# Two reorderings in a hybrid trunk's attention part: first differences of V behind weight splits, and ada sums handed out at other places

## The chip, the cores and the metric

One core of a Trainium2 chip runs the whole program. The metric is the device time of one execution in microseconds (us); three runs of the kernel before gave a median of 1159.88 us (1157.45 to 1161.33). Engines are called by their names: TensorE (PE, with its weight loads PEld), VectorE (DVE), ScalarE (ACT), GpSimd (POOL), and SyncE (SP), which here only issues transfers.

## The reference

The kernel computes two layers on 512 tokens of width 1024, in float32. Layer 0 mixes tokens by stick-breaking attention with 16 heads of 64, layer 1 by a gated token-mixing MLP; each is followed by a SwiGLU block. Every sub-layer has a norm before and behind it and a shift, a scale and a gate computed from a conditioning vector c. The part that matters here:

```python
def ada_modulation(c, w, b):
    m = jax.nn.silu(c) @ w + b
    shift, scale, gate = jnp.split(m, 3, axis=-1)
...
        log_beta = jax.nn.log_sigmoid(z)
        log_1m = jnp.where(before, jax.nn.log_sigmoid(-z), 0.0)
        later = lax.cumsum(log_1m, axis=3, reverse=True) - log_1m
        a = jnp.where(before, jnp.exp(log_beta + later), 0.0)
        outs.append(jnp.einsum('bhts,bhsd->bhtd', a.astype(v.dtype), v[:, :, :kend]))
...
        shift, scale, gate = ada_modulation(c, mix_ada_w[i], mix_ada_b[i])
        h = rms_norm(x, mix_pre_g[i]) * (1.0 + scale) + shift
        y = stick_breaking_mixer(h, sb_w_qkv[j], sb_w_o[j])
        x = x + gate * rms_norm(y, mix_post_g[i])
```

The weights `a` of one row are differences of neighbouring running products of sigmoid(-z). The kernel moves that difference to the other factor: it multiplies the running products with the first differences of V along the tokens.

## The kernel before, in words

**Products in three parts.** A float32 factor is split into a high part that TensorE's fast format holds (`h`, made by ScalarE as a copy) and the rest (`l`, made by VectorE as source minus high part). `mm3` (L104) multiplies high by high, high by low and low by high. Every weight tile of 512 KB goes the same way: SyncE loads it into `raw` (a ring of two buffers), ScalarE makes `wh` (L159, or L154 for the q and k weights of head pairs 1 to 7) and VectorE makes `wl` (L160 or L155) into a ring of five. A `raw` buffer is free for the next load when `wl` has read it. `wget` emits the splits some tiles ahead of use.

**Helpers and lines.** `mm` (L93) records nearly every matmul and `transpose` (L101) the rest. The class `Vector` (L62) passes VectorE's operations on, so most of VectorE's rows have L69; `split` gives ScalarE's rows with L116. While `pe["chain"]` or `dve.chain` is set, each operation on that engine is ordered behind the one before it, so the written order is the executed one. `order` (L85) adds such an order between two instructions without a semaphore.

**Stages around the change.** First come the norm, the turning of h and the ada sums of the first sub-layer (to 61 us or so), mixed with the first half of V (columns 0 to 511) and the q and k of head pair 0. The second half of V follows (the loop over k, L958): eight steps of 12 matmuls (`v_step`), weights for two steps in one tile, with the scores `z` of head pair 0 between them (blocks named B31, B2 and B0). Then 3 + 8 + 9 steps of the filler, then eight head pairs. The filler yields after each eighth of a q or k product for a later pair (banks `pqk`); `fill(n, at)` takes n such steps.

**First differences.** `u_steps` takes the four token tiles of one half of V in the order 2, 3, 0, 1. For each, GpSimd issues a transfer that copies the tile one token up into `vs` (one buffer, L635 and L637); VectorE subtracts (L644); ScalarE and VectorE split the result into U's two parts. The next copy reuses `vs`, so it starts when U's low part is written. The first half's four steps stand in the loop of V's second half, after k = 1, 3, 5 and 7. V's first half is kept for this in `vf`, two tiles of the pool `npool`, which has two buffers; so is the second half afterwards.

**A head pair.** `scores` makes z, ScalarE's sigmoid writes `ga`, and VectorE's scan makes the running products `left`. `flip` transposes them (`tw`), ScalarE and VectorE split them into `ar`, and `values` multiplies with U into `av`. `gather` and `part` make the output `of` and its split `o`. Filler steps stand between these.

**Ada sums.** `Bg` computes a gate G, a scale A and a shift B for coming sub-layers, a stage at a time. There are eight multiply-add stages each on VectorE over 128x1024 (tile `rawada`, loaded by SyncE), then a split of the sum in two halves (`acch`, `accl`) and, after a pause of one stage, two matmuls with ones for each half; here they write into the scores' first bank, `z`. `ada_step` runs the next stage of G and, when G is through, of A and B. G's tiles lie in the pool of 28 slots, A's and B's in a pool with two buffers. Stages are handed out at k = 2, 4, 6, inside `fill(..., 1)` after the second filler step, and once more per pair from pair 4 on; what is left is run after the pairs.

Of the kernel before, what the change touches and what calls it, by code (L numbers as in the profile page):

```python
# [31 lines left out]
def trunk(ctx: ExitStack, tc: tile.TileContext, A: dict, out: bass.AP):  # L32
    nc = tc.nc
# [5 lines left out]
    npool = ctx.enter_context(tc.tile_pool(name="npool", bufs=2))  # L39
# [37 lines left out]
    dve = Vector()  # L77
# [43 lines left out]
    turn = [-1]  # L121
    wpools = [(wpool, 5)]
    fwork = {}

    raws = []

    def wload():

        src, a, b, key = stream[len(raws)]
        if src is None:  # L130
            raws.append(block_loads(key[1]))
            return
        raw = wraw.tile([P, a, b], F32, tag="raw", name=nm("raw"))
        load(raw[:], src)
        raws.append(raw)

    def wemit():
        n = len(got)
        src, a, b, key = stream[n]
        if len(raws) == n:  # L140
            wload()
        if src is None:
            if len(raws) == n + 1 < len(stream) and stream[n + 1][0] is None:
                wload()
            got.append(blocks(*raws[n]))
            return
        raw = raws[n]
        if key[0] == "wdn" and key[2] in SEVEN[key[1]]:
            got.append(down_blocks(raw))
            return  # L150
        h, l = wtile(a, b)
        if key[0] == "wqk" and key[1]:

            act.activation(h[:], raw[:], AF.Copy)  # L154
            nc.vector.tensor_tensor(l[:], raw[:], h[:].bitcast(F32), ALU.subtract)  # L155
            if len(raws) == n + 1 and stream[n + 1][3][0] == "wqk":
                wload()
        else:
            act.activation(h[:], raw[:], AF.Copy)  # L159
            nc.vector.tensor_tensor(l[:], raw[:], h[:].bitcast(F32), ALU.subtract)  # L160
        got.append((h, l))

    def wtile(a, b):
        turn[0] = (turn[0] + 1) % sum(c for _, c in wpools)
        pool = wpools[0][0] if turn[0] < wpools[0][1] else wpools[1][0]
        return (
            pool.tile([P, a, b], F32R, tag="wh", name=nm("wh")),
            pool.tile([P, a, b], F32R, tag="wl", name=nm("wl")),
        )
# [405 lines left out]
    def ada_step(n=1):  # L575
        bg.step(bg0.step(n))
# [42 lines left out]
            a, b = hTk(hT, k, tt * P, P)  # L619
            mm3(vb[tt][:], a, b, w[0][:, k % 2, :], w[1][:, k % 2, :], k == 0, k == KD - 1)  # L620

    def v_evac(vb):
        vf = [npool.tile([P, 2, 512], F32, tag="n", name=nm("vf")) for _ in range(2)]
        vf = [vf[tt // 2][:, tt % 2, :] for tt in range(NT)]
        for tt in range(NT):
            act.activation(vf[tt], vb[tt][:], AF.Copy)
        return vf

    def u_steps(vf, hf, pool):

        def shifted(tt):
            vs = pool.tile([P, 512], F32, tag="vs", name=nm("vs"))
            if tt == NT - 1:
                nc.gpsimd.memset(vs[96:P, :], 0.0)
            nc.gpsimd.dma_start(out=vs[0 : P - 1, :], in_=vf[tt][1:P, :])  # L635
            if tt < NT - 1:
                nc.gpsimd.dma_start(out=vs[P - 1 : P, :], in_=vf[tt + 1][0:1, :])  # L637
            return vs

        turns = (2, 3, 0, 1)  # L640
        vs = shifted(turns[0])
        yield
        for n, tt in enumerate(turns):
            dve.tensor_tensor(vs[:], vs[:], vf[tt], ALU.subtract)  # L644
            src = vs[:].rearrange("p (a e c) -> p a e c", a=4, e=2)
            dst = U[hf][tt][:].rearrange("p a (q c) -> p a q c", q=4)
            split(dst[:, :, 0::3, :], dst[:, :, 1:3, :], src)
            if n + 1 < NT:
                vs = shifted(turns[n + 1])
            yield  # L650
# [75 lines left out]
    vb = [bank("v0") for _ in range(NT)]  # L726
# [36 lines left out]
    act.activation(ones_r, cc[:], AF.Copy)  # L763
    st0.__exit__(None, None, None)
    fwork["raw"] = ctx.enter_context(tc.tile_pool(name="wraw2", bufs=2))
    vf0 = v_evac(vb)
    o8 = []
    with tc.tile_pool(name="att", bufs=1) as att, tc.tile_pool(name="att2", bufs=2) as att2:

# [49 lines left out]
        def fill(n, at=None):  # L819
            for j in range(n):  # L820
                next(fgen, None)
                if at is not None and j == min(at, n - 1):
                    ada_step()


# [3 lines left out]
        for js in (B31, B2, B0):  # L829
            at, n = {}, 0  # L830
# [121 lines left out]
        early_u = u_steps(vf0, 0, att)  # L952
        next(early_u)
        vb = [bank("v1") for _ in range(NT)]
# [3 lines left out]
        for k in range(KD):  # L958
            if k % 2 == 0:
                wv = wget(("wv", 1, k // 2))  # L960
            v_step(vb, 1, k, wv)
            if k in (1, 4):
                cur[0](B31 if k == 1 else B2)
            if k in (2, 4, 6):
                ada_step()
            if k % 2:
                next(early_u)
        late_u = u_steps(v_evac(vb), 1, att)
        next(late_u)
        dve.chain = True  # L970
        tw = [bank("tw") for _ in range(2)]
        av = [bank("av") for _ in range(2)]
        fill(3, 1)
        cur[0](B0)
        for n in FIRST:
            fill(n, 2)
        for i in range(NPAIR):
            scores, flip, values, gather, part = cur
            more = i + 1 < NPAIR
            F = iter(FILLS if i < 5 else LAST[i - 5])  # L980
            flip(LATE, 0)
            flip(LATE, 1)
            if i:
                last_part()
            fill(next(F))
            if more:
                cur = attend(i + 1)
                cur[0](B31)
            fill(next(F), 1)
            values(LATE, 0, False)  # L990
            values(LATE, 1, False)
            fill(next(F))
            flip(EARLY[0], 0)
            flip(EARLY[0], 1)
            if i < 4:
                next(late_u)
            else:
                ada_step()
            fill(next(F))
            if more:  # L1000
                cur[0](B2)
            fill(next(F), 1)
            values(EARLY[0], 0, False)
            values(EARLY[0], 1, False)
            flip(EARLY[1], 0)
            flip(EARLY[1], 1)
            fill(next(F))
            if more:
                cur[0](B0)
            fill(next(F), 1)  # L1010
            values(EARLY[1], 0, True)
            values(EARLY[1], 1, True)
            gather()
            last_part = part
# [521 lines left out]
```

## Time and profile before

| | before |
|---|---|
| median of three runs | 1159.88 us |
| profiled execution, its own time | 1160.02 us |
| its span, first to last instruction | 1158.3 us |
| TensorE busy | 1124.4 us (97%) |
| VectorE busy | 932.9 us (81%) |
| ScalarE busy | 596.5 us (52%) |
| mean granted TensorE clock | 0.992 |

A row of the timeline gives start, duration, engine, line, operation, tile written <- tiles read, shapes and count, and in brackets how long the engine had been idle and what ended that idle time. A row of the waits gives engine, line and tile that waited, what for, the total in us, how often, and the longest. A row of the stretches gives a window, its length, each engine's busy time with its count of instructions, the granted clock (1.00 is full), the DMA engines' busy share and GB/s. Starts are in us from the span's start.

### The profile page before, as it was taken

What the parts mean: (1) busy time and instruction counts of PE and PEld (TensorE: products, weight loads), DVE (VectorE), ACT (ScalarE), POOL (GpSimd) and SP (SyncE); (2) the same over time, 40 slices, a digit from 0 to 9 for tenths busy, and PEclk for the clock granted to TensorE, in tenths of its full rate; (3) what the DMA queues carried; (4) which work ended last, traced back from release to release, by engine and by line L of the source; (5) the groups of instructions that cost most, each with busy time, mean ns of one, the idle gap of its engine ahead of it and who ended that gap; (6) DMA issues with size and microseconds to landing.
All of it is one profiled execution on the core that took longest, in us unless ns stands there. A gap on an engine that the chain in (4) does not pass through costs nothing.

```text
span 1158.3 us, 18661 instructions
## 1 busy us (share of the span) xinstructions
PE 1124.4 (97%) x7436; PEld 1013.5 (88%) x7436; DVE 932.9 (81%) x1215; ACT 596.5 (52%) x985; POOL 30.0 (3%) x55
## 2 busy tenths in 40 slices
PE   6969999999999999999999999999999999999997
PEld 4757878778999999998878898988999999999996
DVE  4956899976998988869686965668979898789996
ACT  6434566565665555555142633526545555565652
POOL 0011010000000000000000000000000000000000
PEclk9979999999999999999999999999999999999999
DMA  8844343513424444337887375224243433222242
GB/s 309 332 150 168 119 155 118 164 55 127 164 92 138 136 135 139 128 110 258 282 281 257 141 251 168 92 76 161 95 143 128 149 133 124 89 92 91 92 151 105
DMA packets 51644, 176.52 MB, mean 152 GB/s; under 512 B 6106, under 2 KB 9434, under 8 KB 51556
## 3 DMA queue, kind: packets, MB, share of 16 engines
q1 hardware_dynamic: 48996, 166.94, 42.7%
q0 software_dynamic: 2560, 8.39, 2.0%
q8 instruction: 58, 0.95, 0.3%
q14 instruction: 30, 0.25, 0.1%
HBM read 164.82 MB, written 8.39 MB: 150 GB/s over the span
## 4 chain that ended last, share of the span: by engine, by line
PE 84%; DMA 6%; DVE 5%; ACT 2%; issue 2%; SPq 0%; POOL 0%; DVEq 0%; ACTq 0%; POOLq 0%
PE r L93 33%; PE y L93 10%; PE v L93 7%; PE pqk L93 6%; PE gu L93 5%; PE u L93 4%; PE X L93 4%; DMA rawada<-in_ada 4%; PE Y L93 3%; PE z L93 2%; PE av L93 2%; PE W L93 1%; PE Z L93 1%; PE tp L101 1%; PE tw L101 1%
## 5 line engine op out<-in xcount | busy, mean ns | idle before, releaser
L93 PE MATMUL r<-Sl,wh 128*128 128x256 f32 x608 | 172.4, 283 | 0.0
L93 PE MATMUL r<-Sh,wh 128*128 128x256 f32 x608 | 172.3, 283 | 0.0
L93 PE MATMUL r<-Sh,wl 128*128 128x256 f32 x608 | 172.3, 283 | 0.0
L93 PE MATMUL y<-wh,as 128*128 128x512 f32 x480 | 150.8, 391 | 0.0
L159 ACT ACTIVATE wh<-raw 128x1024 fp32r<-128x1024 f32 x87 | 91.7, 1058 | 114.7 <-PE y L93 57.4
L116 ACT ACTIVATE wh<-f 128x1024 fp32r<-128x1024 f32 x87 | 92.2, 1060 | 91.2 <-PE r L93 66.5
L69 DVE TENSOR_TENSOR wl<-f,wh 128x1024 fp32r<-128x1024 f32 x87 | 106.4, 1223 | 40.0 <-ACT wh L116 40.0
L160 DVE TENSOR_TENSOR wl<-raw,wh 128x1024 fp32r<-128x1024 f32 x87 | 105.9, 1220 | 35.4 <-ACT wh L159 35.2
L93 PEld LDWEIGHTS r<-Sh,wl 128*128 128x128 f32 x608 | 116.9, 192 | 0.0
L93 PEld LDWEIGHTS r<-Sh,wh 128*128 128x128 f32 x608 | 116.9, 192 | 0.0
L93 PEld LDWEIGHTS r<-Sl,wh 128*128 128x128 f32 x608 | 116.9, 192 | 0.0
L93 PEld LDWEIGHTS y<-wh,as 128*128 128x128 f32 x480 | 90.1, 188 | 19.0 <-DVE G L69 0.5
L93 PE MATMUL y<-wl,as 128*128 128x512 f32 x240 | 93.8, 391 | 0.0
L93 PE MATMUL r<-hTh,wh 128*128 128x256 f32 x304 | 87.9, 292 | 0.0
L93 PE MATMUL r<-hTl,wh 128*128 128x256 f32 x304 | 85.5, 283 | 0.0
L93 PE MATMUL r<-hTh,wl 128*128 128x256 f32 x304 | 81.1, 283 | 0.0
L93 PE MATMUL r<-hTh,b 128*128 128x256 f32 x304 | 61.0, 283 | 0.0
L93 PE MATMUL v<-wh,hTh 128*128 128x512 f32 x128 | 52.7, 411 | 7.7 <-ACT wh L159 5.9
L93 PEld LDWEIGHTS r<-hTh,wh 128*128 128x128 f32 x304 | 58.0, 191 | 2.4 <-DVE gu L69 0.6
L93 PEld LDWEIGHTS r<-hTl,wh 128*128 128x128 f32 x304 | 58.1, 191 | 0.1
L116 ACT ACTIVATE wh<-rawx 128x1024 fp32r<-128x1024 f32 x38 | 40.3, 1060 | 34.7 <-PE r L93 31.8
L93 PEld LDWEIGHTS r<-hTh,wl 128*128 128x128 f32 x304 | 56.0, 191 | 0.0
(268 smaller groups left out, 2985.0 us busy)
## 6 DMA issues: line engine op xcount, KB each, us to landing
rawada<-in_ada SPq DMA_DIRECT2D x80, 512.0 KB, 4.5
rawy<-in_wy SPq DMA_DIRECT2D x38, 512.0 KB, 3.6
rawx<-in_wx SPq DMA_DIRECT2D x38, 512.0 KB, 4.1
raw<-in_wdown SPq DMA_DIRECT2D x22, 512.0 KB, 4.8
raw<-in_wdn SPq DMA_DIRECT2D x22, 512.0 KB, 3.5
raw<-in_wqk SPq DMA_DIRECT2D x16, 512.0 KB, 3.5
ada<-in_ada0p SPq DMA_DIRECT2D x12, 512.0 KB, 8.0
raw<-in_wgu SPq DMA_DIRECT2D x12, 512.0 KB, 3.6
```

Of the source, the lines that this page charges most:

```text
L69: b = getattr(nc.vector, op)(*args, **kw)
L93: b = nc.tensor.matmul(o, l, r, start=start, stop=stop, skip_group_check=True)
L101: last_tp[0] = nc.tensor.transpose(o, i, ident)
L116: act.activation(hi, src, AF.Copy)
L159: act.activation(h[:], raw[:], AF.Copy)
L160: nc.vector.tensor_tensor(l[:], raw[:], h[:].bitcast(F32), ALU.subtract)
```

## The change

Three things are changed. Outside the chained stretch each first difference is now ordered behind `last_low`, the latest `wl` of a weight tile made on L160 (new L161); the first half's steps stand after k = 3, 5, 7 and after the loop. V's first half lies in two of the 28 slots; the second half stays in `npool`. Ada stages are handed out at k = 1, 2, 6, four times in each of the two long fills ahead of the first pair (`FIRST`, after filler steps 0, 2, 4 and 6), twice per pair in pairs 0 to 3 and three times from pair 4 on (where the pair has filler steps there). Before these were one in each long fill, three per pair, and four from pair 4 on.

```diff
         else:
             act.activation(h[:], raw[:], AF.Copy)
-            nc.vector.tensor_tensor(l[:], raw[:], h[:].bitcast(F32), ALU.subtract)
+            last_low[0] = nc.vector.tensor_tensor(l[:], raw[:], h[:].bitcast(F32), ALU.subtract)
...
-    def v_evac(vb):
-        vf = [npool.tile([P, 2, 512], F32, tag="n", name=nm("vf")) for _ in range(2)]
+    def v_evac(vb, tile2):
+        vf = [tile2() for _ in range(2)]
...
-            dve.tensor_tensor(vs[:], vs[:], vf[tt], ALU.subtract)
+            b = dve.tensor_tensor(vs[:], vs[:], vf[tt], ALU.subtract)
+            if not dve.chain:
+                order(b, last_low[0])
...
-    vf0 = v_evac(vb)
+    vf0 = v_evac(vb, lambda: slot(F32, "vf"))
...
-                if at is not None and j == min(at, n - 1):
+                if at is not None and j in [min(a, n - 1) for a in at]:
                     ada_step()
...
-            if k in (2, 4, 6):
+            if k in (1, 2, 6):
                 ada_step()
-            if k % 2:
+            if k in (3, 5, 7):
                 next(early_u)
-        late_u = u_steps(v_evac(vb), 1, att)
+        next(early_u)
+        late_u = u_steps(
+            v_evac(vb, lambda: npool.tile([P, 2, 512], F32, tag="n", name=nm("vf"))), 1, att
+        )
...
-        fill(3, 1)
+        fill(3, (1,))
         cur[0](B0)
         for n in FIRST:
-            fill(n, 2)
+            fill(n, (0, 2, 4, 6))
...
             if i < 4:
                 next(late_u)
-            else:
-                ada_step()
...
-            fill(next(F), 1)
+            fill(next(F), (1,) if i > 3 else ())
```

More of the change, by code (lines that the diff above doesn't have):

```diff
@@ L123, in trunk @@
     fwork = {}
+    last_low = [None]
     raws = []
@@ L988, in trunk @@
                 cur[0](B31)
-            fill(next(F), 1)
+            fill(next(F), (1,))
             values(LATE, 0, False)
@@ L1001, in trunk @@
                 cur[0](B2)
-            fill(next(F), 1)
+            fill(next(F), (1,))
             values(EARLY[0], 0, False)
@@ L1009, in trunk @@
                 cur[0](B0)
-            fill(next(F), 1)
+            fill(next(F), (1,) if i > 3 else ())
             values(EARLY[1], 0, True)
```

## The prediction

> **What bounds the kernel now.** I read the page first, then TensorE's waits, then the stretches, then each engine's rows where TensorE stands still. From the page, its first lines and the chain of work that ended last:
>
> ```profile
> span 1158.3 us, 18661 instructions
> PE 1124.4 (97%) x7436; PEld 1013.5 (88%) x7436; DVE 932.9 (81%) x1215; ACT 596.5 (52%) x985; POOL 30.0 (3%) x55
> ...
> PE 84%; DMA 6%; DVE 5%; ACT 2%; issue 2%; SPq 0%; POOL 0%; DVEq 0%; ACTq 0%; POOLq 0%
> ```
>
> TensorE is busy 97% of the span and makes up 84% of the chain, so a change pays or costs only where TensorE itself stands. The two longest waits in TensorE's list that lie in the attention part:
>
> ```profile
> PE v L93 <- ACT wh L159: 5.9, 1, 5.9
> PE v L93 <- DVE wl L160: 3.2, 1, 3.2
> ```
>
> The stretches (columns: PE, PEld, DVE, ACT, POOL busy, granted clock, DMA share, GB/s):
>
> ```profile
> 71.50:82.00 10.50, 1.38 (x4) 0.74 (x3) 7.82 (x8) 4.87 (x9) 1.08 (x2) 0.60 0.08 25
> 82.00:101.00 19.00, 19.00 (x76) 15.08 (x76) 10.09 (x12) 7.36 (x11) 2.07 (x4) 0.86 0.62 207
> 126.00:203.00 77.00, 77.00 (x467) 62.05 (x466) 73.41 (x82) 46.60 (x90) 4.09 (x7) 1.00 0.43 140
> 203.00:263.00 60.00, 55.10 (x337) 43.33 (x336) 47.96 (x58) 33.20 (x62) 0.00 (x0) 1.00 0.32 106
> ```
>
> There are two soft places. From 71.5 to 82 us TensorE works 1.38 of 10.5 us, and the next stretch runs at a mean clock of 0.86. From 203 to 263 us (the last three head pairs) it stands 60 - 55.10 = 4.9 us. Between them (126 to 203) TensorE is never idle although VectorE is busy 73.41 of 77 us: a late start there isn't made up.
>
> The first hole in rows, TensorE, then VectorE, then ScalarE:
>
> ```profile
> 70.50 1.13 PE L93 MATMUL z<-k,q 64*128 64x128 f32 x12
> 77.56 0.80 PE L93 MATMUL v<-wh,hTh 128*128 128x512 f32 x1 [5.92 <-ACT wh L159]
> 81.55 0.79 PE L93 MATMUL v<-wl,hTh 128*128 128x512 f32 x1 [3.20 <-DVE wl L160]
> 82.14 0.63 PE L93 MATMUL v<-wh,hTl 128*128 128x512 f32 x1
> ...
> 87.75 0.39 PE L93 MATMUL v<-wl,hTh 128*128 128x512 f32 x1
> ...
> 101.23 0.39 PE L93 MATMUL pqk<-hTh,wh 128*128 128x512 f32 x1
> ...
> 106.67 0.39 PE L93 MATMUL z<-accl,ones 128*128 128x512 f32 x1
> ...
> 122.34 1.08 PE L93 MATMUL av<-ar,U 128*128 128x128 f32 x8
> ```
>
> ```profile
> 71.12 0.69 DVE L69 TENSOR_TENSOR vs<-vs,vf 128x512 f32<-128x512 f32 x1 [4.63 <-DMA vs<-vf]
> ...
> 77.48 0.69 DVE L69 TENSOR_TENSOR vs<-vs,vf 128x512 f32<-128x512 f32 x1 [2.68 <-DMA vs<-vf]
> 78.09 2.29 DVE L69 TENSOR_TENSOR_SCAN left<-ga,ones 128x1027 f32<-128x1027 f32 x1
> 80.30 1.20 DVE L160 TENSOR_TENSOR wl<-raw,wh 128x1024 fp32r<-128x1024 f32 x1
> 81.41 0.69 DVE L69 TENSOR_TENSOR U<-vs,U 128x512 fp32r<-128x512 f32 x1
> ...
> 87.08 0.69 DVE L69 TENSOR_TENSOR vs<-vs,vf 128x512 f32<-128x512 f32 x1 [3.85 <-DMA vs<-vf]
> ...
> 96.65 0.68 DVE L69 TENSOR_TENSOR U<-vs,U 128x512 fp32r<-128x512 f32 x1
> ...
> 118.11 1.03 DVE L69 SCALAR_TENSOR_TENSOR ar<-tw,ar 128x384 fp32r<-128x384 f32 x2 [0.94 <-ACT ar L906]
> ```
>
> ```profile
> 75.38 1.19 ACT L885 ACTIVATE ga<-z 128x128 f32<-128x128 f32 x4
> 76.43 1.08 ACT L159 ACTIVATE wh<-raw 128x1024 fp32r<-128x1024 f32 x1
> 78.21 0.63 ACT L116 ACTIVATE U<-vs 128x512 fp32r<-128x512 f32 x1 [0.70 <-DVE vs L69]
> ...
> 99.39 1.28 ACT L626 ACTIVATE vf<-v 128x512 f32<-128x512 f32 x2 [2.17 <-PE v L93]
> ```
>
> The scores z end at 71.6. The next matmuls of V need weights made in two instructions, `wh` on ScalarE and `wl` on VectorE. ScalarE's `wh` (76.43) stands behind `ga` and the ada sum's split, which stand behind U's split, which waits for VectorE's first difference (71.12), late because its shifted copy came by DMA. VectorE's `wl` (80.30) stands behind the second difference (77.48, another shifted copy) and the scan (78.09). TensorE gets `wl` at 81.55.
>
> **Part 1: the differences go behind the weights.** In the changed program VectorE's row is: last two sums of G, `wl` (k=2,3), scan, `wl` (k=4,5), `wl` (k=6,7), first difference; ScalarE has the ada split, three `ga`, `wh`. All these inputs are there by 71.6 (in the window from 71.5 the DMA is busy only 0.08 of the time). So `ga` starts at 71.7; three of four take 0.9 of the 1.19 us; `wh` 1.08 to 73.7; `wl` 1.20 to 74.95. TensorE goes on at 74.95 instead of 81.55: **-6.6 us** there. From 81.55 to 101.23 V takes 19.7 us, 2.7 of it by the half clock (0.43 us between starts at 82.14, 0.23 at 87.75). Its granted clock:
>
> ```profile
> 73.00:74.00 1.00, 0.00 (x0) 0.82 0.00 0
> ...
> 87.00:88.00 1.00, 1.00 (x6) 0.86 0.23 94
> ```
>
> It fell at about 73.6, 2 us after the last z, and rose at 87.3, 5.7 us after work was back. I take the same 19.7 us: V ends at 94.6. The Trainium skill, "TensorE: Matmul & The Clock Gate", section "Part 1: The HAM clock gate", has the half clock come after one idle window of about 3.4 us. The hole would now be 3.3 us, so by that rule the clock might stay up and V end at an estimated 91.9. This trace differs, since the clock was down 2 us after work ended, and the measurement decides.
>
> **What is late next.** The four differences still form a serial chain, because the shifted copy has one buffer (`vs`): its next copy may start only when U's lower half has been written. Rows of the GpSimd queue:
>
> ```profile
> 73.72 0.52 POOL L634 MEMSET vs<- 32x512 f32 x1 [8.50 <-DVE U L69]
> ...
> 82.40 0.54 POOL L635 DMA_DIRECT2D vs<-vf  x1 [7.31 <-DVE U L69]
> ```
>
> Both rows waited for U. From the end of a U (81.41 + 0.69 = 82.1) to the next difference (87.08) is 5.0 us; for the second copy, from the memset that its U released (73.72) to 77.48, 3.8 us. The tile view of the four copies has this line:
>
> ```profile
> DMA to landing us min/median/max: 2.9/4.2/6.8
> ```
> The last step must also come before what stands next on VectorE: in the changed program the fourth U (lower half) is followed by `accl` (lower half of the G sum), the B0 scan, then the two products into G. In the old order the fourth U ended at 97.3 (96.65 + 0.68), long before TensorE wanted `accl`. Now, with each `wh`/`wl` where the changed row has it, and a raw tile landed 4.0 us after its issue, a middle of these medians (the last column):
>
> ```profile
> raw<-in_wqk SPq DMA_DIRECT2D x14, 512.0 KB, 3.5
> rawada<-in_ada SPq DMA_DIRECT2D x13, 512.0 KB, 4.0
> ...
> raw<-in_wv SPq DMA_DIRECT2D x3, 512.0 KB, 4.2
> ...
> g<-in_post_g SPq DMA_DIRECT2D x1, 512.0 KB, 6.4
> ```
>
> - last V `wl`: raw issued 74.95, landed 79.0, `wh`, `wl` (1.1 and 1.2) to 81.2. First difference to 81.9; a pair `wl` comes between (raw issued at 78.3, landed 82.3, `wh` 83.4, `wl` 84.6); first U to 85.2.
> - second copy there 85.3 + 3.8 = 89.1; the scan of B2 and a `wl` keep VectorE to 89.5; difference, `wl` 1.2, U 0.7: 91.9.
> - third: 91.9 + 5.0 = 96.9; difference 97.6, `wl` 98.7, U 99.4.
> - fourth: 99.4 + 5.0 = 104.4; difference 105.05, ScalarE's half 0.63, U 0.69: 106.3; `accl` 0.68: **107.0**.
>
> TensorE needs that `accl` much earlier than before. It is read by the two matmuls z<-acch, z<-accl, which sit in its fixed order: in the old program after 18 matmuls of the next pair (106.67 the second), in the new one after 12, because sums are now handed out at the first fill of eight. That place is reached at 94.6 + (106.67 - 101.23) - 6 x 0.227 = 98.7. So TensorE stands from 98.7 to 107.0: **the 6.6 us are gone, a wait of 8.3 us takes the place of the one removed.** Against the old 106.67 it is late by 0.3 + 1.4 (the six matmuls not yet done) = **+1.7 us**.
>
> **Part 2: eight sums ahead of the first pair.** Three terms follow.
>
> *Second G half.* VectorE after 107.0: scan 2.29, product 0.67, `accl` 0.68: 110.5. TensorE would be there at 107.2 + 6 x 0.227 = 108.6: **+1.9 us**.
>
> *Clock.* After 8 us idle it is at half again. With 5.7 us of low clock from 107.0 on, most of it inside the wait just counted, four matmuls at 0.43 instead of 0.23 and the two sums are left: **+1.1 us**. So far +4.7: the first `av<-ar` would go from 122.34 to 127.0.
>
> *The A sums.* Two stages of A's sum (tiles loaded long ago) and four more now stand on VectorE before the first `ar`, which `av` waits for; before, none did (the first is after the third scan). The four read tiles from a pool of two buffers, so the third load is issued only when the first sum has read its tile, and lands 4.0 us later. Walked: pair 1's q weights, whose tiles the next ones reuse, are used up at 113.1 (110.9 and six matmuls, four of them slow); `wh`, `wl`, q to 116.1; sums 1, 2 to 118.5 (1.2 each, as in the rows of part 3); `wl` 120.9 (its tile free when k's 24 matmuls end, 118.6); sum 3 at 117.3 + 4.0, to 122.5; sum 4 to 123.8; k 0.7 to 124.5; sum 5 at 122.5 + 4.0, to 127.8; sum 6 to 129.0; the two `ar` 1.03, the first at 129.5. Against 127.0 **+2.5 us**; av starts 129.6 instead of 122.34: **+7.2 us in all**. From the nearest rows the two loads could take 3.5 (wqk) or 4.0 us each: 1.0 less at best; were all hidden, 0.
>
> The queues: SP's load of A's bias row stands behind the memset on GpSimd, itself behind the fourth copy (about 102), and pair weights stand behind it on SP; those wait for the q `wl` at 115.5 anyway, so 0; without that cover it would add up to its 6 us. G's row takes 6.4 us from about 99, there at 105, ahead of 109: 0, up to 1.5 if slower.
>
> **Part 3: fewer sums in the pairs.** Pairs 0 to 3 lose VectorE work while TensorE is full: 0. In the stretch where TensorE stands 4.9 us, two B sums go (five to three between the scans). In the view of the chain both are on it (start, us, what):
>
> ```profile
> 215.66 1.18 DVE B L69
> ...
> 223.96 0.64 DVE B L69
> ```
>
> Two at a pitch of 1.2 us: **-2.4 us**. Bounds: 0 (another wait steps in) and -4.9 (all of TensorE's idle).
>
> **Part 4: V's first half in two slots of the 28** instead of the two-buffer pool. ScalarE's copies of the second half waited for TensorE (row 99.39), not for the buffer: 0. Against it a slot could be missed; no row shows one: at most one copy step, 0.7. The extended list in `fill` costs nothing on the chip.
>
> **Sum.** +7.2 - 2.4 = +4.8. The profiled execution took 1160.02 us (span 1158.3), 0.1 above the median of 1159.88. Predicted: 1160.0 + 4.8 = **1164.8 us**. With the end's bounds: 1162.3 to 1167.2. By the Trainium skill's clock rule the B2 scan would come 2.7 us earlier and the chain of differences about 0.5: an estimated 1164.3.
>
> **Rivals.**
> 1. *The sums' loads are hidden.* The A term falls away (+4.7 - 2.4): 1162.3, no measurable change. For it: only 2.5 us to cover, and 3.5 us landings exist. Against: six sums in a row, with two buffers.
> 2. *Faster: the chain of differences keeps up.* TensorE doesn't wait at 98.7, keeps 6.6 and 2.4: 1151.0. It decides when `accl` is ready by 98.7, so the three copies (3.8 + 5.0 + 5.0 = 13.8) would have to take 5.5 together. Three of the shortest landing, 2.9 us, are 8.7. With the old `wl` between them gone too, the chain still ends near 103.6; half-way cases end near no change. By the Trainium skill's clock rule it would be an estimated 1148.3.
> 3. *Slower copies and nothing back at the end.* The longest landing was 6.8 us against a median of 4.2, with other loads under way. With 1.8 more on the fourth copy, on which G's row and two weights fall, and no gain at the end: 1160.0 + 7.2 + 1.8 = 1169.0. Against it: the last pairs' chain does run through the B sums.
> 4. *The order isn't as asked*, differences stay ahead of the weights: 1160. The new order names that `wl` outright; small, inside the range.
>
> **How the numbers follow.** Forecast 0.50; loads hidden (with 4) 0.27; chain keeps up 0.12; slower copies 0.11. About 0.3% (3.5 us) is what a measurement of this kernel can tell from no change: above 1163.4 is slower, below 1156.4 faster. So faster 0.12, same 0.27, slower 0.61. The range leaves out rival 2 and part of 3: 1159.5 to 1169.5; the likeliest alone is 1162.3 to 1167.2.
>
> **What would show it.** Right: TensorE resumes V near 75 and ends V at 92 to 95; a new wait of z for `accl` of 6 to 11 us up to about 107, a second dip of the clock, the first av at 127 to 131; the last three pairs with 1 to 4 us idle. Wrong: z finds `accl` ready, `ar` is on time, or the last pairs stand as before.

## The result, and the profile after

The changed kernel takes 1165.63 us (median of eight runs, 1161.67 to 1170.29) against 1158.86 us for the kernel before on the same chip (eight runs, 1157.12 to 1162.70): a ratio of 1.0057, 95% interval 1.0034 to 1.0080. It is slower. 1164.8 was predicted.

The first lines of the page of the changed kernel and the first of TensorE's list of waits (columns: total us, times, longest us):

```profile
span 1163.7 us, 18665 instructions
PE 1126.9 (97%) x7436; PEld 1015.0 (87%) x7436; DVE 933.8 (80%) x1215; ACT 596.9 (51%) x985; POOL 30.0 (3%) x55
...
PE 80%; DMA 8%; DVE 7%; ACT 3%; issue 2%; SPq 0%; DVEq 0%; POOL 0%; ACTq 0%
```

```profile
PE z L93 <- DVE accl L69: 8.6, 1, 8.6
```

Each engine's busy time is that of before within 3 us. In the chain the share of the DMAs has grown from 6% to 8%, that of VectorE from 5% to 7%. The two long waits for V's weights (5.9 and 3.2 us) have shrunk to 2.0 and 0.8 (in the brackets of the rows at 70.60 and 71.86 below), and a new one stands on top: 8.6 us for `accl`.

TensorE's rows of the changed kernel, to be read beside those of before:

```profile
67.48 1.13 PE L93 MATMUL z<-k,q 64*128 64x128 f32 x12
70.60 0.51 PE L93 MATMUL v<-wh,hTh 128*128 128x512 f32 x1 [1.98 <-ACT wh L160]
71.86 0.80 PE L93 MATMUL v<-wl,hTh 128*128 128x512 f32 x1 [0.76 <-DVE wl L161]
...
91.74 0.39 PE L93 MATMUL pqk<-hTh,wh 128*128 128x512 f32 x1
...
97.05 0.50 PE L93 MATMUL z<-acch,ones 128*128 128x512 f32 x1 [1.32 <-ACT ga L888]
106.12 0.80 PE L93 MATMUL z<-accl,ones 128*128 128x512 f32 x1 [8.57 <-DVE accl L69]
...
109.70 0.63 PE L93 MATMUL z<-accl,ones 128*128 128x512 f32 x1
...
129.53 0.22 PE L93 MATMUL av<-ar,U 128*128 128x128 f32 x1
131.07 1.08 PE L93 MATMUL av<-ar,U 128*128 128x128 f32 x7 [1.32 <-DVE ar L69]
```

The two executions do not reach the first scores at the same time (70.50 before, 67.48 here); the last section says why. Times below are therefore also given from the start of the first z<-k,q. From there TensorE resumes V with `wl` after 4.4 us (before 11.05), ends V after 24.3 (30.7), has the `accl` product after 38.6 (36.2), and starts the first av after 62.05 (51.84), seven eighths of it another 1.3 us later because the next `ar` was late too. Up to the first av the gain of 6.5 us has become a loss of 10.2 to 11.5 us.

VectorE's rows of the changed kernel between, and GpSimd's issues of the shifted copies:

```profile
70.58 1.23 DVE L161 TENSOR_TENSOR wl<-raw,wh 128x1024 fp32r<-128x1024 f32 x1 [5.88 <-ACT wh L160]
...
77.51 0.68 DVE L69 TENSOR_TENSOR vs<-vs,vf 128x512 f32<-128x512 f32 x1
...
88.30 0.68 DVE L69 TENSOR_TENSOR U<-vs,U 128x512 fp32r<-128x512 f32 x1
...
95.16 0.69 DVE L69 TENSOR_TENSOR vs<-vs,vf 128x512 f32<-128x512 f32 x1 [2.33 <-DMA vs<-vf]
...
96.90 0.69 DVE L69 TENSOR_TENSOR U<-vs,U 128x512 fp32r<-128x512 f32 x1
103.39 0.69 DVE L69 TENSOR_TENSOR vs<-vs,vf 128x512 f32<-128x512 f32 x1 [5.81 <-DMA vs<-vf]
104.78 0.69 DVE L69 TENSOR_TENSOR U<-vs,U 128x512 fp32r<-128x512 f32 x1 [0.69 <-ACT U L116]
105.39 0.68 DVE L69 TENSOR_TENSOR accl<-G,acch 128x512 fp32r<-128x512 f32 x1
...
108.77 0.68 DVE L69 TENSOR_TENSOR accl<-G,acch 128x512 fp32r<-128x512 f32 x1
...
115.27 2.59 DVE L69 SCALAR_TENSOR_TENSOR A<-rawada,sc,A 128x1024 f32<-128x1024 f32 x2
...
121.58 2.60 DVE L69 SCALAR_TENSOR_TENSOR A<-rawada,sc,A 128x1024 f32<-128x1024 f32 x2 [1.32 <-DMA rawada<-in_ada]
...
127.95 2.60 DVE L69 SCALAR_TENSOR_TENSOR A<-rawada,sc,A 128x1024 f32<-128x1024 f32 x2 [3.17 <-DMA rawada<-in_ada]
130.47 1.01 DVE L69 SCALAR_TENSOR_TENSOR ar<-tw,ar 128x384 fp32r<-128x384 f32 x2
```

```profile
89.28 0.54 POOL L636 DMA_DIRECT2D vs<-vf  x1 [6.34 <-DVE U L69]
...
97.88 0.54 POOL L636 DMA_DIRECT2D vs<-vf  x1 [7.56 <-DVE U L69]
98.41 0.51 POOL L638 DMA_DIRECT2D vs<-vf  x1
```

The third and the fourth copy are issued when U's low part releases the one tile `vs` (89.28 after the U of 88.30, 97.88 after the U of 96.90), and the difference that reads them follows 5.9 and 5.5 us later (95.16, 103.39). VectorE sat idle for the copies for 2.33 and 5.81 us, and `accl` stands right behind the fourth. Further down it waited 1.32 and 3.17 us for tiles of the A sum, ahead of the first `ar`.

The stretches of the changed kernel, the first hole and the last three head pairs (60 us from about 80 us after the first av, as in the rows of before; the experiments' last pairs are read the same way):

```profile
68.50:79.00 10.50, 7.76 (x22) 5.81 (x21) 6.37 (x5) 4.62 (x8) 0.00 (x0) 0.67 0.36 105
210.00:270.00 60.00, 58.24 (x358) 46.86 (x357) 48.18 (x60) 36.62 (x68) 0.00 (x0) 1.00 0.26 88
```

In the last pairs TensorE now stands 60 - 58.24 = 1.76 us, 3.1 less than before (4.9). From the first scores to the end of the span the sum is +11.5 - 3.1 = +8.4 us: 1163.7 - 67.48 = 1096.2 against 1158.3 - 70.50 = 1087.8. The first scores came 3.0 us earlier in this execution, so the span itself grew by 5.4.

### The profile page after: what moved, and what is told of

The parts are those of the page before. It is cut to its first block, busy times and chain, and to the rows that moved or that the text cites. A ratio compares the mean times of both kernels' runs of the same rounds, so it can differ in the third digit from the quotient of the medians.

```text
span 1163.7 us, 18665 instructions
## 1 busy us (share of the span) xinstructions
PE 1126.9 (97%) x7436; PEld 1015.0 (87%) x7436; DVE 933.8 (80%) x1215; ACT 596.9 (51%) x985; POOL 30.0 (3%) x55
## 4 chain that ended last, share of the span: by engine, by line
PE 80%; DMA 8%; DVE 7%; ACT 3%; issue 2%; SPq 0%; DVEq 0%; POOL 0%; ACTq 0%
PE r L93 32%; PE y L93 8%; PE v L93 8%; PE pqk L93 6%; DMA rawada<-in_ada 5%; PE X L93 4%; PE gu L93 4%; PE Y L93 3%; PE u L93 3%; PE z L93 2%; PE av L93 2%; PE W L93 1%; PE Z L93 1%; PE tw L101 1%; DVE wl L161 1%
## 5 line engine op out<-in xcount | busy, mean ns | idle before, releaser
L160 ACT ACTIVATE wh<-raw 128x1024 fp32r<-128x1024 f32 x87 | 91.6, 1058 | 113.3 <-PE y L93 58.3
L161 DVE TENSOR_TENSOR wl<-raw,wh 128x1024 fp32r<-128x1024 f32 x87 | 105.8, 1219 | 43.0 <-ACT wh L160 42.6
L116 ACT ACTIVATE wh<-f 128x1024 fp32r<-128x1024 f32 x87 | 92.2, 1060 | 91.0 <-PE r L93 66.5
L93 PE MATMUL v<-wh,hTh 128*128 128x512 f32 x128 | 51.6, 403 | 3.8 <-ACT wh L160 2.0
```

The costliest lines, as they stand in the source:

```text
L93: b = nc.tensor.matmul(o, l, r, start=start, stop=stop, skip_group_check=True)
L116: act.activation(hi, src, AF.Copy)
L161: last_low[0] = nc.vector.tensor_tensor(l[:], raw[:], h[:].bitcast(F32), ALU.subtract)
```

## The experiments

The theory after the result: the explicit order starts the first difference some 9 us after the scores end (77.51 against 68.6); four copies through one tile cannot then be done when TensorE wants the gates' low part; the eight sums cost a little more at the first av. Rivals were that the sums are the whole loss, that the order gains nothing anyway, and that the slots for V matter. The edits are given against the kernel named. Where a run gives "after the first z", it is worked out from its rows as above. Each ratio compares with the kernel before on the run's own chip. There the kernel before took 1159.49 us (for the first two experiments below and the two with the copies apart), 1161.30 us (for the changed kernel without its order and the two combinations) or 1160.36 us (for the other four). So a difference between the times of two of these groups, or of one of them and the changed kernel, can be off by 1 to 2 us, and the ratio is the better guide.

**The order and the slots without the sums** (against the kernel after):

```diff
-            if k in (1, 2, 6):
+            if k in (2, 4, 6):
...
-            fill(n, (0, 2, 4, 6))
+            fill(n, (2,))
...
+            else:
+                ada_step()
...
-            fill(next(F), (1,) if i > 3 else ())
+            fill(next(F), (1,))
```

> The change without its second part: first differences behind the weights and V's first half in slots, ada sums handed out as before. Theory (the serial chain of four shifted copies makes the low half of G's sum late): TensorE takes up V's second half 6.6 us earlier, then waits 8 to 10 us in the two sum matmuls after 18 matmuls of the next pair; with the half clock behind it the first av comes about 5 us later than before and nothing is won in the last pairs: about 1164 us, ratio 1.003 to 1.006. Rival (the wait comes from handing the sums out early): the 6.6 us are kept, about 1153 us, ratio 0.993 to 0.996.

1164.73 us, ratio 1.0048 (1.0032 to 1.0065). TensorE's row:

```profile
105.27 0.80 PE L93 MATMUL z<-accl,ones 128*128 128x512 f32 x1 [8.68 <-DVE accl L69]
```

The wait for `accl` is there with the sums handed out as before, 8.68 us long, and the first av comes 56.97 us after the first z, 5.1 later than before. The last pairs stand idle 4.95 us as before. As expected.

**The sums without the order** (against the kernel after; the slots stay):

```diff
-            if not dve.chain:
-                order(b, last_low[0])
...
-            if k in (3, 5, 7):
+            if k % 2:
...
-        next(early_u)
```

> The change without its first part: sums handed out as in the changed kernel, the differences ordered as before. Theory: V's second half resumes as late as before, G's low half is there in time, but the six A sums ahead of the first ar wait twice for tiles (4.9 us each) and bring the first av 5 to 7 us later; the last pairs give back 3: about 1163 us, ratio 1.001 to 1.005. Rival (the sums ahead of the pairs cost nothing): only the 3 us of the last pairs are seen, about 1156 us, ratio 0.996 to 0.999.

1154.94 us, ratio 0.9959 (0.9940 to 0.9977): faster than before, where a loss was expected. A miss. The profile showed TensorE resuming V 5.8 us after the first z although no order was asked for, and no wait for `accl`. What did that in this kernel was open. It still had V's first half in slots, and so the slots were the next suspect.

**The slots alone** (against the kernel before):

```diff
-    def v_evac(vb):
-        vf = [npool.tile([P, 2, 512], F32, tag="n", name=nm("vf")) for _ in range(2)]
+    def v_evac(vb, tile2):
+        vf = [tile2() for _ in range(2)]
...
-    vf0 = v_evac(vb)
+    vf0 = v_evac(vb, lambda: slot(F32, "vf"))
...
-        late_u = u_steps(v_evac(vb), 1, att)
+        late_u = u_steps(
+            v_evac(vb, lambda: npool.tile([P, 2, 512], F32, tag="n", name=nm("vf"))), 1, att
+        )
```

> The kernel before with one of the change's parts alone: V's first half is evacuated into slots instead of the shared pool (no explicit order, no new hand-out of sums). Its built VectorE order already has the low parts of V's third and fourth weights right after the first shift-and-mix, ahead of the scan and the second difference. Theory (the gain of the run with the sums alone came from this order, not from the sums): TensorE resumes V about 5.8 us after the first z instead of 11.05, the gathered gates' low part is in time, and the time is 1152 to 1156. Rival A (slots cost and bring nothing, as the prediction has it): 1158.5 to 1160.5. Rival B (the earlier order brings the late gates with it, as in the changed kernel): a wait of 5 us or more for the low part of the gates, and 1160 or more.

1154.17 us, ratio 0.9948 (0.9929 to 0.9968). VectorE's rows of this run:

```profile
69.88 0.69 DVE L69 TENSOR_TENSOR vs<-vs,vf 128x512 f32<-128x512 f32 x1 [4.10 <-DMA vs<-vf]
71.31 0.69 DVE L69 TENSOR_TENSOR U<-vs,U 128x512 fp32r<-128x512 f32 x1 [0.74 <-ACT U L116]
72.97 1.23 DVE L160 TENSOR_TENSOR wl<-raw,wh 128x1024 fp32r<-128x1024 f32 x1 [0.96 <-ACT wh L159]
74.11 2.29 DVE L69 TENSOR_TENSOR_SCAN left<-ga,ones 128x1027 f32<-128x1027 f32 x1
76.32 1.20 DVE L160 TENSOR_TENSOR wl<-raw,wh 128x1024 fp32r<-128x1024 f32 x1
77.43 0.69 DVE L69 TENSOR_TENSOR vs<-vs,vf 128x512 f32<-128x512 f32 x1
...
91.91 0.69 DVE L69 TENSOR_TENSOR accl<-G,acch 128x512 fp32r<-128x512 f32 x1
```

Nothing but the place of two tiles is changed, and the order that the program is built in is another: `wl` for V's third step now stands after the first U and ahead of the scan and the second difference, which the kernel before had the other way round (77.48, 78.09, 80.30). ScalarE's `wh` comes earlier too. In the kernel before, the last two multiply-adds of G ran behind the first difference, and the split `acch`, which waited for them, stood ahead of `ga` and `wh` (75.38, 76.43):

```profile
73.53 1.28 DVE L69 SCALAR_TENSOR_TENSOR G<-rawada,sc,G 128x1024 f32<-128x1024 f32 x1
74.84 0.63 ACT L116 ACTIVATE acch<-G 128x512 fp32r<-128x512 f32 x1 [2.32 <-DVE G L69]
```

With the slots the split is done before the scores:

```profile
65.81 0.63 ACT L116 ACTIVATE acch<-G 128x512 fp32r<-128x512 f32 x1 [1.98 <-DVE G L69]
71.87 1.07 ACT L159 ACTIVATE wh<-raw 128x1024 fp32r<-128x1024 f32 x1
```

TensorE resumes 5.7 us after the first z, and its waits there are 3.3 and 0.5 us. The first differences still begin ahead of the weights, so `accl` (91.91) is early. The first av is 46.17 us after the first z, 5.7 sooner than before. The theory of this run holds: this part, costed at 0, is worth 6 us by itself.

**The changed kernel without its explicit order** (two lines against the kernel after):

```diff
-            if not dve.chain:
-                order(b, last_low[0])
```

> The changed kernel with its explicit order alone undone (the two lines that put the first differences of V's first half behind the second weight's low part); the sums, the steps and the slots stay. Theory (the explicit order is the whole loss: it starts the chain of four copies some 6 us later than it could start, and with one tile for the copies this lands on the low part of the gates): the first difference runs before that low part, TensorE resumes about 5.8 us after the first z instead of 4.4, its wait for the gates' low part is under 1 us, and the time is 1153 to 1156, some 10 below the changed kernel. Rival (the sums and the steps handed out differently cost too, whatever the order): 1158 to 1163.

1154.30 us, ratio 0.9949 (0.9933 to 0.9965). TensorE's and VectorE's rows of this run:

```profile
66.62 1.13 PE L93 MATMUL z<-k,q 64*128 64x128 f32 x12
70.94 0.79 PE L93 MATMUL v<-wh,hTh 128*128 128x512 f32 x1 [3.19 <-ACT wh L160]
72.20 0.79 PE L93 MATMUL v<-wl,hTh 128*128 128x512 f32 x1 [0.47 <-DVE wl L161]
...
95.69 0.40 PE L93 MATMUL z<-accl,ones 128*128 128x512 f32 x1
```

```profile
67.83 0.69 DVE L69 TENSOR_TENSOR vs<-vs,vf 128x512 f32<-128x512 f32 x1 [4.01 <-DMA vs<-vf]
...
70.92 1.23 DVE L161 TENSOR_TENSOR wl<-raw,wh 128x1024 fp32r<-128x1024 f32 x1 [0.96 <-ACT wh L160]
...
89.88 0.68 DVE L69 TENSOR_TENSOR accl<-G,acch 128x512 fp32r<-128x512 f32 x1
```

The first difference (67.83) is back ahead of the weights, V resumes 5.6 us after the first z, and no `accl` is waited for. Two lines make 1165.63 - 1154.30 = 11.3 us (by the ratios 1.1%, some 12.5 us): they gain 1.2 us at the first hole (5.6 against 4.4) and lose some ten times that at `accl`. With the sums as before the same two lines and their steps make 1164.73 - 1154.17 = 10.6 us (by the ratios 1.0%, some 11.6 us). The sums and the steps do not matter to that; the rival falls.

**The four copies apart** (against the kernel after, and against the first experiment):

```diff
-            vs = pool.tile([P, 512], F32, tag="vs", name=nm("vs"))
+            vs = pool() if callable(pool) else pool.tile([P, 512], F32, tag="vs", name=nm("vs"))
...
-        early_u = u_steps(vf0, 0, att)
+        early_u = u_steps(vf0, 0, lambda: slot(F32, "vs", 1, 512)[:, 0, :])
```

> The changed kernel with one edit: the four shifted copies of V's first half go to four tiles of the slot pool, so no copy waits for the U before it. Theory: the low half of G's sum is ready about 100 (on the clock of before) instead of 109, the wait of z for it shrinks from 8.6 to 0 to 2.5 us, the second dip of the clock goes; A's sums still wait for their tiles: 6 to 8 us faster than the changed kernel, about 1158 us, ratio to before 0.997 to 1.001. Rival (the wait hangs on the last weight of the five that must wait for V's end, not on the copies): stays at 1163 to 1166 us.

> The differences behind the weights, sums as before, and the four copies apart. Theory: nothing is late behind V's second half, the 6.6 us stay: about 1153 us, ratio 0.993 to 0.996, with no wait of z for accl above 1.5 us and no second dip of the clock. Rival (the chain of differences costs as much on VectorE wherever its copies lie): 1159 us or more.

The first takes 1155.97 us, ratio 0.9972 (0.9957 to 0.9987), the second 1151.79 us, ratio 0.9943 (0.9924 to 0.9963). TensorE's row of `accl` in the first of them, and the line of its copies in the view of that tile:

```profile
100.34 0.50 PE L93 MATMUL z<-accl,ones 128*128 128x512 f32 x1 [0.75 <-DVE accl L69]
```

```profile
DMA to landing us min/median/max: 1.5/6.6/7.4
```

With a tile for each, a copy no longer waits for the U before it. One takes longer (median 6.6 us, in the kernel before 4.2), yet TensorE waits 0.75 us for `accl` in place of 8.57. So it is the one tile that turned the order into a loss, and not the copies' own length: 1165.63 - 1155.97 = 9.7 us with the sums ahead, 1164.73 - 1151.79 = 12.9 with the sums as before. Between these two runs only the sums differ, and the one with eight sums ahead is 4.2 us slower: its first av is some 7 us later (52.5, taking the wait between its first and the other seven products into account, against 45.45 after the first z), and its last pairs give 3.1 back (58.22 us busy against 55.10).

**The copies apart without the order** (against the kernel before: the slots and the copies apart):

```diff
...
-            vs = pool.tile([P, 512], F32, tag="vs", name=nm("vs"))
+            vs = pool() if callable(pool) else pool.tile([P, 512], F32, tag="vs", name=nm("vs"))
...
-    vf0 = v_evac(vb)
+    vf0 = v_evac(vb, lambda: slot(F32, "vf"))
...
-        early_u = u_steps(vf0, 0, att)
+        early_u = u_steps(vf0, 0, lambda: slot(F32, "vs", 1, 512)[:, 0, :])
...
```

> The kernel before with V's first half in slots and the four shifted copies in four slots of their own, without the explicit order. Its built VectorE order has the third weight's low part behind the second difference. Theory (the price of the change's order is that all four copies and sums are done one after the other, and the copies apart end that): no wait for the low part of the gates; the copies' own place costs nothing; 1152 to 1156. If the explicit order is what is worth something beside it, this run is 1 to 3 us above the 1151.8 of the order with copies apart; if it equals it within 1 us, the order brings nothing that the slots don't.

1152.84 us, ratio 0.9939 (0.9919 to 0.9958). TensorE resumes V after 5.4 us instead of 4.4 with the order, and its first av comes after 46.06 us against 45.45. By the traces the order is then worth 0.6 us; the intervals of the two times cover each other, so the times do not show it.

**Three of the sums earlier** (against the order with copies apart):

```diff
-            if k in (2, 4, 6):
+            if k in (1, 2, 4, 6):
...
-            fill(n, (2,))
+            fill(n, (2, 6))
```

> The fastest kernel so far (the order, the copies apart, the sums as before) with three of the adaLN sums handed out earlier: one more at a step of the weights' loop and one more in the first block of filling, so three fewer at the last head pairs. Theory (the changed kernel's sums cost at the first av because eight of them must pass through two load tiles there; three do not fill that path, and the last pairs, which give back some 3 us for eight, give back 1 to 2): 1149.5 to 1152, the first av no more than 1.5 us later. Rival (each sum ahead of the first head pair costs what it costs in the changed kernel, 7.3/8 or about 0.9 us, against 0.4 given back): 1153 to 1154.

1152.42 us, ratio 0.9936 (0.9915 to 0.9956). A miss in its mechanism: the first av is 49.48 us after the first z, 4.0 later than with the sums as before. Most of it is one new wait of TensorE, with 3.4 us at half clock behind it (granted 0.50 from 100.6 to 104.0):

```profile
95.68 0.39 PE L93 MATMUL z<-accl,ones 128*128 128x512 f32 x1
...
99.53 0.96 PE L93 MATMUL z<-k,q 64*128 64x512 f32 x6 [2.77 <-DVE G L69]
```

The small sums came ahead of B0's scores, which then wait for the bank `z` until the product into G has read it. The last pairs give back 2.4 us (57.46 busy). What it gains at the end it has spent ahead of the first av.

**The sums' tiles in slots** (against the kernel after with the copies apart):

```diff
-    bg0, bg = Bg("G0", slots=3, gap=1), Bg("A0", "B0", lag=1, gap=1)
+    bg0, bg = Bg("G0", slots=3, gap=1), Bg("A0", "B0", slots=3, lag=1, gap=1)
```

> The changed kernel with the copies apart, and besides with the sums' loads in slots, so that a load need not wait until one of two tiles is free. Theory (what the eight sums cost ahead of the first av is the two-tile path of the loads: VectorE waited 1.3 and 3.2 us there for them in the changed kernel): VectorE's waits for these loads there fall under 1 us, the first av comes 2 to 5 us earlier than with the copies apart alone (50.05 us after the first z), and the time is 1151 to 1154. Rival (it is VectorE's own 2.6 us a sum): waits fall and the first av stays within 1 us, 1155 to 1157.

1151.31 us, ratio 0.9933 (0.9911 to 0.9955). VectorE's waits for these tiles with the copies apart alone, and then the line of the loads in the view of the DMAs of either run (columns: times, KB each, median us from issue to landing):

```profile
DVE A L69 <- DMA rawada<-in_ada: 3.8, 4, 2.4
```

```profile
rawada<-in_ada SPq DMA_DIRECT2D x7, 512.0 KB, 4.0
```

```profile
rawada<-in_ada SPq DMA_DIRECT2D x9, 512.0 KB, 8.4
```

In the second run VectorE's list has no such wait, although a load now takes 8.4 us in place of 4.0. They are issued some 10 us before they are read (the first at 94.0, its sum at 104.5). The first av comes 47.82 us after the first z, but part of that is luck: in this execution the clock stayed at half for 3.4 us after the first scores, and for 6.8 us in the two runs with the copies alone apart. So V took 18.42 us from its `wl` to its end, against 19.78 with the eight sums ahead and 19.89 with the sums as before. With the same clock the first av would come at about 49.2, an estimate. Of the 7 us that eight sums cost there, some 3.3 was then the two tiles, and some 3.8 is left, about as much as the 3.1 that the end gives back. (One sum is 1.3 us of VectorE; the rows of 2.6 us hold two.) The times agree: with or without the eight sums the ratio is the same within its interval (0.9933, 0.9943).

**Two combinations.** No order, with copies and sums' tiles in slots (against the run with the sums without the order):

```diff
-    bg0, bg = Bg("G0", slots=3, gap=1), Bg("A0", "B0", lag=1, gap=1)
+    bg0, bg = Bg("G0", slots=3, gap=1), Bg("A0", "B0", slots=3, lag=1, gap=1)
...
-            vs = pool.tile([P, 512], F32, tag="vs", name=nm("vs"))
+            vs = pool() if callable(pool) else pool.tile([P, 512], F32, tag="vs", name=nm("vs"))
...
-        early_u = u_steps(vf0, 0, att)
+        early_u = u_steps(vf0, 0, lambda: slot(F32, "vs", 1, 512)[:, 0, :])
```

> Eight sums ahead of the first head pair, no explicit order, and copies and sums' loads each in slots. Theory (the order gains nothing once the copies have tiles of their own; the eight sums cost little ahead of the first av once their loads are not gated, and the last pairs give back 3 us): 1149 to 1152, equal to the 1151.3 of the same with the order within 2 us. If the order is worth its 1.0 to 1.4 us of earlier resumption, this run is that much above: 1152 to 1153.

The order, three sums earlier, and both kinds of tiles in slots (against the run with three sums earlier, the first two lines of this diff alone):

> The order, copies apart, three sums earlier, and the sums' loads in slots. In the run with three sums earlier TensorE waited 2.77 us for the gathered gates G ahead of the third shift's rows, because the small sum moved ahead; that is not touched here. Theory (with loads in slots three sums earlier still cost this wait, and the last pairs give back less than with eight): 1151 to 1153, not below the 1151.3 of eight sums. Rival (fewer sums ahead are cheaper): 1149 to 1151.

They took 1152.75 us, ratio 0.9933 (0.9913 to 0.9953), and 1153.76 us, ratio 0.9951 (0.9934 to 0.9968). In the first TensorE resumes V 6.0 us after the first z against 4.4, its first av is at 49.50 against 47.82. Its ratio is the same as with the order (0.9933), and the intervals reach 0.2% to either side, so the times do not say whether the order is worth 1 us. The second came out a little above the 1151 to 1153 that its theory had. The wait of 2.77 us for G is there again, as expected, and slots for the loads bring nothing with three sums.

All together:

| kernel | us | ratio to before (95%) | V resumes after first z | first av after first z | last pairs idle |
|---|---|---|---|---|---|
| before | 1158.86 | 1 | 11.05 | 51.8 | 4.9 |
| after | 1165.63 | 1.0057 (1.0034-1.0080) | 4.4 | 62.1 to 63.4 | 1.8 |
| order and slots, sums as before | 1164.73 | 1.0048 (1.0032-1.0065) | 4.4 | 57.0 | 4.9 |
| sums and slots, no order | 1154.94 | 0.9959 (0.9940-0.9977) | 5.8 | 51.6 to 52.7 | 1.8 |
| after without the order's two lines | 1154.30 | 0.9949 (0.9933-0.9965) | 5.6 | 51.3 to 52.0 | 1.8 |
| slots alone | 1154.17 | 0.9948 (0.9929-0.9968) | 5.7 | 46.2 | 4.9 |
| after, copies apart | 1155.97 | 0.9972 (0.9957-0.9987) | 4.4 | 50.1 to 52.5 | 1.8 |
| order, slots, copies apart | 1151.79 | 0.9943 (0.9924-0.9963) | 4.4 | 45.5 | 4.9 |
| slots, copies apart, no order | 1152.84 | 0.9939 (0.9919-0.9958) | 5.4 | 46.1 | 4.9 |
| order, slots, copies apart, three sums earlier | 1152.42 | 0.9936 (0.9915-0.9956) | 4.4 | 49.5 | 2.5 |
| after, copies and sums' tiles apart | 1151.31 | 0.9933 (0.9911-0.9955) | 4.4 | 47.8 | 1.8 |
| the same without the order | 1152.75 | 0.9933 (0.9913-0.9953) | 6.0 | 49.5 | 1.8 |
| three sums earlier, copies and sums' tiles apart | 1153.76 | 0.9951 (0.9934-0.9968) | 4.4 | 49.6 | 2.5 |

In the rows with the sums' tiles apart 0.9 to 1.4 us of the first av is the shorter time at half clock.

The fastest ones beat the kernel before by 0.6 to 0.7% and the changed one by 1.2% (1151.31 against 1165.63); the runs do not rank them among themselves.

## Why the prediction was right, and where its terms were off

- *What bounds the kernel: two soft places, the rest full.* Right. TensorE is busy all 77 us of the stretch between in the changed kernel too, and what was late at the first av stayed lost until the last pairs.
- *Part 1, TensorE goes on 6.6 us earlier.* Right: 71.86 - 67.48 + 70.50 = 74.9 on the clock of before, against 74.95 predicted; V ends at 94.8 against 94.6. But the prediction gives all of it to the order. With V's first half in slots and no order V already resumes 5.7 us after the first z, so of the 6.7 us (11.05 to 4.4) the order made 1.3 and the slots 5.4.
- *What is late next, `accl`.* The mechanism is right, and it is shown by the copies apart and by taking the two lines back. The size was short by 2 us: `accl` is used at 109.1 on the clock of before, not at 107.0. The mis-sized term is "91.9 + 5.0" and "99.4 + 5.0": from the end of U to the next difference the trace has 6.2 and 5.8 us, as the last issue of the fourth copy begins 0.8 us after U (98.41 against 96.90 + 0.69) and the difference reads it 5.0 us later. The wait of 8.6 against 8.3 agrees only because TensorE reached it later too: it waited 1.32 us for `ga` just before (97.05).
- *Part 2, second G half +1.9 and clock +1.1.* Only their sum is borne out. TensorE's granted clock was 0.50 from 106 to 112, and at that pace it reached the second `accl` (109.70) just as VectorE had made it (109.45), so no wait shows. The slow clock took the place of the wait.
- *Part 2, the A sums +2.5.* Right in its cause, too small: VectorE waited 1.32 + 3.17 us for two loads. From the end of a pair's first sum (115.27 + 1.3, 121.58 + 1.3) to the pair that reads the load it issued are 5.0 and 5.1 us, where 4.0 was taken. TensorE also waited for k (1.74 us) and for the second `ar` (1.32 us), which no term had. The two runs with the copies apart put the sums at 7 us at the first av, where the terms for the second G half and the A sums make 4.4.
- *Part 3, -2.4.* It measures -3.1, in every run with the new sums (58.2 us busy against 55.1). Which waits make the 0.7 us beyond the two B sums was not followed.
- *Part 4, 0.* This step failed as an account of a part: V's first half in slots changes the order in which the program is built, and alone makes the kernel 6 us faster. The forecast didn't suffer, because Part 1 was walked along the order of the changed program, in which the explicit order overrides that. But "the change loses 4.8" is then made of a part that gains 6 us and a part that loses 11 to 12, which the sum did not see.
- *The sum.* +7.2 at the first av became +10.2 to 11.5, and -2.4 became -3.1: +8.4 in place of +4.8 from the first scores on. The profiled execution had 3.0 us less ahead of them. By the medians it is 1165.63 - 1158.86 = +6.8 us, in the range. That the time came within 0.8 us of 1164.8 is luck: the sum was 2.0 us too small, and the base of 1160.0 stood 1.1 us above the 1158.86 measured with it.
- *The rivals.* "The chain of differences keeps up" needed `accl` ready at 98.7; it was ready at 109.1. "The loads are hidden" is refuted by VectorE's rows. "Slower copies" was right in its first half (1 us each, not 1.8 on one) and wrong that the end gives nothing.

In the prediction the clock rule of the Trainium skill ("TensorE: Matmul & The Clock Gate", section "Part 1: The HAM clock gate": down after an idle window of about 3.4 us) would have let the clock stay up in the shorter hole. The changed kernel's trace differs: with a matmul at 70.60 inside the hole, and no idle time longer than 1.98 us, the granted clock is 0.62 from 71 to 72 and 0.50 from 72 to 78.

## What to carry to other kernels

When an instruction is put behind another to let that one go first, follow what the late one feeds: here it was the head of a chain of four transfers through one buffer, and for the 1.2 us that the order gained at the front the kernel lost some 11 us net at the end of the chain. Give the chain its own buffers first, then order; and after any edit of buffers read the order that was built, since a change of a tile's place alone moved VectorE's work and was worth more than the reordering asked for. The waits for loads that pass through two buffers went away here by issuing the loads earlier: with more buffers each took twice as long and nobody waited. And before two traces are compared at one point, see whether the clock was low for as long in both: here that alone moved the first av by 1.4 us.

## What the runs showed of the hardware

The time up to the first scores varied by 4 us between executions of programs whose work up to there is nearly the same: z<-k,q began between 66.5 and 70.8 us in the thirteen profiled executions. A part of it is the granted clock. The stretch from 30 to 40 us, in the kernel before and in the changed kernel:

```profile
30.00:40.00 10.00, 8.93 (x39) 7.31 (x38) 9.64 (x14) 4.52 (x6) 1.42 (x2) 0.83 0.84 311
```

```profile
30.00:40.00 10.00, 8.95 (x45) 7.45 (x44) 9.67 (x14) 3.63 (x5) 1.42 (x2) 1.00 0.83 318
```

TensorE is busy 8.9 us of it in both and waits there once, for about 1.05 us (until 36.32 before, until 34.76 after). In four of the thirteen executions the clock fell to half after this hole (mean 0.83 or 0.84), in nine it did not; the first scores of the four began at 70.1 to 70.8, of the nine at 66.5 to 68.7. The rest of the spread comes from earlier, and what makes it was not followed. So a hole of 1 us can halve the clock or not where the work is the same, and for how long it stays low varies too: after the first scores it was back 5.7 us after work in the kernel before (81.55 to 87.3), 6.2 us in the changed one (71.86 to 78.1), and 3.1 us in the run with copies and sums' tiles in slots (71.75 to 74.8). Counted from the fall of the clock there is a pattern. Between 28 and 135 us the thirteen traces show 25 stretches at half clock, and each lasts 3.4, 6.8, 10.2 or 13.7 us, once to four times 3.41: in the kernel before 36.09 to 39.50 and 73.63 to 87.28, in the changed one 71.23 to 78.06, 98.54 to 112.19 and 125.84 to 129.26. None of them ends in between, though work was back at different moments. The page of the Trainium skill named above says that the windows run freely and that the point of transition therefore varies; these traces agree with that, and differ from its idle window.

Transfers of one size did not have one length: a 254 KB copy within the chip landed after 2.8 to 7.7 us, a 512 KB load of the sums after a median of 4.0 us with two tiles and 8.4 us when slots let more of them be issued ahead. The Trainium skill ("DMA: Bandwidth & Descriptors", section "Anatomy of one DMA — SWDGE (gpsimd) path") gives 2 us and the bytes at 436 GB/s, an estimate of 2.6 us for the copy; the copies of the chain in the changed kernel took about twice that (median 5.2 us).
